# Modulation of a four-block network: sums along features on partitions, with the first block's value projection fed by pairs of features

## The chip, the cores and the metric

The kernel runs on one core of one Trainium2 chip. The metric is the device time of one execution in microseconds (us); the time of the kernel before is the median of three runs, 1766.88 us (1766.28 to 1769.8).

## The reference, cut to what matters

Four blocks (GLA, SGU, FoX, GLA) run over x, 256 tokens by 1024 features; a hybrid block and a PEER feed-forward follow and are not touched. Each of the four blocks is modulated by a vector worked out from a condition c:

```
cond = silu(c)
for i in range(4):
    mod = cond @ w_mod[i] + b_mod[i]          # w_mod[i]: 1024 x 3072
    shift, scale, gate = split(mod, 3)
    h = rms_norm(x, norm_pre_g[i]) * (1 + scale) + shift
    o = mixer_i(h)                            # starts with h @ w_in
    x = x + gate * rms_norm(o, norm_post_g[i])
```

So each block needs three vectors of 1024 (scale and shift at its start, gate at its end), each a product of a 1024-vector with a 1024 x 1024 matrix of 4 MB. Block 0 begins with the values `v = h @ w_v` (1024 x 1024), then keys, part of the gate z, queries, and the rest of z; a decay is worked out from h through a projection of rank 16.

## The kernel before, in words

**Layout.** h is kept with features on partitions, as 8 tiles (kt) of 128 features by 256 tokens. A float32 product is made of three matmuls of float32r parts: a weight tile of 512 KB (`wr`, 4 buffers) is loaded by SP's queue, copied by ScalarE to a high part `wh` (L203), and VectorE subtracts to get the low part `wl` (L204); `hH` and `hL` are the two parts of h. `w_next` hands out the next weight tile of a fixed plan and splits tiles up to five ahead of it (`LEAD`). `w_split` loads the tile four further on (`RAW`).

**Modulation.** `w_mod` is cut into 96 chunks of 512 KB, twelve parts of 8. A chunk has 128 input features on partitions and 1024 outputs along the row. `m_step` (L242) adds one chunk, times one column of silu(c), into an accumulator of 128 x 1024 on VectorE: L255 for the first chunk of a part, L257 for the other seven. The sum over the 128 partitions is left to `m_cols` (L261): four matmuls with ones (L269, each runs as two), a copy to rows on ScalarE (L308), two transposes (L317), and small VectorE operations that add the bias (L275) and apply the norm's gain (L278, L280). The result `modc` has features on partitions, 8 columns.

**Order.** The program writes every engine's queue by hand. `tick()` runs one step of each generator in `tasks`, then of each in `later`; it is called after each block of a projection. In block 0 the 24 chunks for gate 0, scale 1 and shift 1 are spread over the ticks by the list in L636; `m_load` (L240) loads a chunk two ahead, on the SP queue that carries the weights too.

**Start.** The 16 chunks for scale 0 and shift 0 are loaded first (L1502 to L1537), x, the identity and tri in between. `start()` normalises x and transposes it (L365, L371, L1525, L1527). When all 16 are summed and both `m_cols` are through, h is scaled and shifted (L1548 on ScalarE for hH, L1549 on VectorE), L1550 makes hL, and `gla` begins with `proj_tm` for the values: two groups of 512 columns, each over two token blocks with 4 x 6 matmuls (L426 to L428).

**Behind it.** `decay()` (L598) is a task with seven steps: L604 and L606 (rank-16 projection), L613, `log_sigmoid` (L529 to L536), the running sum L617, L619, and exponentials of differences (L622 to L630). It starts at the fourth tick of the value projection. The keys (4 blocks of 24 matmuls, L409 to L411), two blocks of z (silu, L562), and the queries follow; `c_q` (L647) writes a pair of query blocks with the decay's factor `eq`, `k_scale` (L660) scales the keys, and `mix` makes scores (L671, L673, L675) and outputs. `out_proj` (L477) transposes the gate's columns with a broadcast (L492) at its first tick.

```
while have["k"] < 2 * hp + 2 or have["q"] < 2 * hp + 2:
    yield
```

is what holds the scores of a pair of heads (in `mix`).

Of the kernel before, what the change touches and what calls it, by code (L numbers as in the profile page):

```python
# [16 lines left out]
P = 128  # L17
# [27 lines left out]
def _layout():  # L45
    o = 0
    for name, n in [("g_pre", 32), ("g_post", 32), ("b_mod", 96), ("c", 8), ("b_a", 8),
                    ("g_head", 16), ("gate_bias", 16), ("conv_w", 24), ("norm_mix", 8),
                    ("norm_ffn", 8), ("g_q", 1), ("g_k", 1), ("b_f", 1)]:
        COLS[name] = o  # L50
        o += n
    return o
# [11 lines left out]
def _build(ctx, nc, tc, I, out, dbg):  # L64
# [32 lines left out]
    def add(gen, to=tasks):  # L97
        to.append(gen)
# [24 lines left out]
    x = keep.tile([P, NTB, D], F32, name="x")  # L123
    ident = keep.tile([P, P], F32, name="ident")
    tri = const.tile([P, 384], F32, name="tri")
# [14 lines left out]
    sc = const.tile([P, KT], F32, name="sc")  # L140
    act(sc, col("c", 0, 8), AF.Silu)
# [13 lines left out]
    for l in range(4):  # L155
        if l in (0, 3):
            j = l // 3
            plan_tm(I["gla_v"][j], 2)
# [37 lines left out]
    def w_split(i):  # L196
# [10 lines left out]
        w_load(i + RAW)  # L207
# [14 lines left out]
    mods = {}  # L222
    mctx = ExitStack()
    mpool = mctx.enter_context(tc.tile_pool(name="mpool", bufs=3))
    SHIFT, SCALE, GATE = 0, 1, 2
    mplan = [(0, SCALE), (0, SHIFT), (0, GATE), (1, SCALE), (1, SHIFT), (1, GATE), (2, SCALE), (2, SHIFT),
             (2, GATE), (3, SCALE), (3, SHIFT), (3, GATE)]
    mchunks = [(l, part, kt) for l, part in mplan for kt in range(KT)]
    mraw = {}
    nxt_m = [0]  # L230
    MFIRST = 2 * KT

    def m_load(i):
        if i < len(mchunks):
            l, part, kt = mchunks[i]
            if i < MFIRST and i % 2:
# [5 lines left out]
    def m_step():  # L242
# [6 lines left out]
        if kt == 0:  # L249
            mods[l, part, "acc"] = mpool.tile([P, D], F32, tag="macc", name="macc", bufs=2)  # L250
        acc = mods[l, part, "acc"]
        if i >= MFIRST:
            m_load(i + 2)
        if kt == 0:
# [3 lines left out]
        if kt == KT - 1:  # L258
            add(m_cols(l, part), later)

    def m_cols(l, part):  # L261
        acc = mods.pop((l, part, "acc"))
        mc = tiny.tile([P, 8], F32, tag=f"modc{part}", name="modc", bufs=2)
        mods[l, part] = mc
        for _ in range(2 if part == SHIFT else 4):
            yield
        p = pm()
        for g in range(4):
            mm(p[32 * g:32 * g + 32, 0:S], ones[:, 0:32], acc[:, g * S:(g + 1) * S], start=True, stop=True)  # L269
        yield  # L270
        R = rows_copy(p, 4)
        for _ in range(1 if part == SHIFT else 2):
            yield
        pcv = rows_to_cols(p, 4, R)
        tt(mc.rearrange("p (g t) -> p t g", t=2), pcv.rearrange("p t (g r) -> p t g r", r=32)[:, :, :, 0],  # L275
           col("b_mod", l * 24 + part * 8, 8).rearrange("p (g t) -> p t g", t=2), op=ALU.add)
        if part == SCALE:
            stt(mc, mc, 1.0, col("g_pre", l * 8, 8), op0=ALU.add, op1=ALU.mult)  # L278
        elif part == GATE:
            tt(mc, mc, col("g_post", l * 8, 8), op=ALU.mult)  # L280
# [136 lines left out]

    def proj_tm(n, H, L, consume, early=False, late=None):


        def part(p, w, c, tb):
            wh, wl = w
            tsl = slice(tb * P, (tb + 1) * P)
            for k in range(2):
                kt = c * 2 + k
                mm(p, H[:, kt, tsl], wh[:, k], start=(kt == 0), stop=False)  # L426
                mm(p, H[:, kt, tsl], wl[:, k], start=False, stop=False)  # L427
                mm(p, L[:, kt, tsl], wh[:, k], start=False, stop=(kt == KT - 1))  # L428
# [145 lines left out]
    def gla(l, hs, lp, nA, nB, nF):  # L574
# [23 lines left out]
        def decay():  # L598
            for _ in range(3):
# [1083 lines left out]
```

## Time and profile before

| | us |
|---|---|
| median of 3 runs | 1766.88 |
| the profiled execution | 1772.7 |
| its span on the core | 1770.6 |
| TensorE busy | 1682.3 (95%) |
| VectorE busy | 1284.5 (73%) |
| ScalarE busy | 973.6 (55%) |
| low parts of weights, L204 (VectorE, 504 times) | 614.3 |
| modulation chunks of the page's w_mod loads (88 of SP's 512 KB loads) | 5.5 median to landing |

The busy time of TensorE is modelled and pipelined, so 95% is not 95% of its peak. In the profile "idle before <- releaser" names what ended the idle time of the engine just before an instruction. The granted clock is TensorE's, as a share of 2.4 GHz.

### The profile page before, as it was taken

The numbers are of one execution on the slowest core, as the hardware profiler recorded it, in microseconds if no ns is written. First come the engines' busy times: TensorE is split into PE (matmuls) and PEld (weight loads), VectorE is DVE, ScalarE is ACT, GpSimd is POOL, SyncE is SP. The second block draws the span as 40 slices with busy tenths as digits, with TensorE's granted clock in tenths as the row PEclk, the third lists the DMA queues.
The fourth block names the chain that finished last, engine by engine and source line by source line (L and its number), as shares of the span: only waits on it lengthen the run. The fifth ranks groups of instructions, "written<-read, shape, count | busy, mean of one in ns | idle before, by whom it ended". The sixth has DMA issues, their size and how long they took to land.

```text
span 1770.6 us, 28535 instructions
## 1 busy us (share of the span) xinstructions
PE 1682.3 (95%) x10774; PEld 1485.2 (84%) x10774; DVE 1284.5 (73%) x2589; ACT 973.6 (55%) x1531; POOL 60.6 (3%) x102
## 2 busy tenths in 40 slices
PE   3998999999899999989999999999999999999997
PEld 2886886877698788879979999998999888888886
DVE  7888697877786765674576889997774466666665
ACT  3635445655555544435454446668994555555554
POOL 0000000000000000000000000000000000000000
PEclk8999999999999999999999999999999999999999
DMA  8775885853563555334553766664447677777774
GB/s 331 237 270 178 285 308 164 308 194 132 176 202 123 189 179 170 116 106 157 178 193 114 231 215 201 199 188 151 154 153 236 213 243 236 235 236 235 236 235 160
DMA packets 104188, 357.08 MB, mean 202 GB/s; under 512 B 12273, under 2 KB 13297, under 8 KB 103794
## 3 DMA queue, kind: packets, MB, share of 16 engines
q1 hardware_dynamic: 97200, 335.52, 58.8%
q0 software_dynamic: 5120, 16.78, 2.4%
q10 hardware_dynamic: 1730, 2.96, 0.5%
q8 instruction: 85, 1.39, 0.3%
q14 instruction: 53, 0.43, 0.1%
HBM read 337.38 MB, written 17.83 MB: 201 GB/s over the span
## 4 chain that ended last, share of the span: by engine, by line
PE 78%; DVE 12%; ACT 3%; DMA 3%; issue 3%; POOL 0%; SPq 0%; DVEq 0%; POOLq 0%; ACTq 0%
PE pm L1470 20%; PE pj L1447 6%; PE pj L1445 6%; PE pj L1446 6%; PE pj L426 5%; PE pj L428 5%; PE pj L427 5%; DVE wl L204 4%; PE pj L409 4%; PE pj L410 4%; PE pj L411 4%; PE pm L1352 3%; DMA wmod<-in_w_mod 2%; DVE macc L257 2%; ACT wh L203 1%
## 5 line engine op out<-in xcount | busy, mean ns | idle before, releaser
L204 DVE TENSOR_TENSOR wl<-wr,wh 128x1024 fp32r<-128x1024 f32 x504 | 614.3, 1223 | 308.0 <-ACT wh L203 307.1
L203 ACT ACTIVATE wh<-wr 128x1024 fp32r<-128x1024 f32 x504 | 528.2, 1055 | 216.3 <-PE pm L1470 56.0
L1445 PE MATMUL pj<-uH,wh 128*128 128x256 f32 x1024 | 293.8, 287 | 0.0
L1447 PE MATMUL pj<-uL,wh 128*128 128x256 f32 x1024 | 290.0, 283 | 0.0
L1446 PE MATMUL pj<-uH,wl 128*128 128x256 f32 x1024 | 289.9, 283 | 0.0
L409 PE MATMUL pj<-hH,wh 128*128 128x256 f32 x768 | 225.9, 294 | 0.1
L410 PE MATMUL pj<-hH,wl 128*128 128x256 f32 x768 | 221.0, 288 | 3.2 <-DVE wl L204 3.2
L411 PE MATMUL pj<-hL,wh 128*128 128x256 f32 x768 | 220.3, 287 | 0.0
L1470 PE MATMUL pm<-wh 128*128 128x512 f32 x512 | 202.9, 396 | 4.1 <-ACT wh L325 4.1
L1470 PE MATMUL pm<-wl,wh 128*128 128x512 f32 x512 | 202.6, 396 | 0.0
L1470 PE MATMUL pm<-wh,wl 128*128 128x512 f32 x512 | 202.5, 396 | 0.0
L1445 PEld LDWEIGHTS pj<-uH,wh 128*128 128x128 f32 x1024 | 196.7, 192 | 0.0
L1446 PEld LDWEIGHTS pj<-uH,wl 128*128 128x128 f32 x1024 | 196.4, 192 | 0.1
L1447 PEld LDWEIGHTS pj<-uL,wh 128*128 128x128 f32 x1024 | 196.2, 192 | 0.0
L426 PE MATMUL pj<-wh,hH 128*128 128x512 f32 x352 | 144.9, 412 | 15.5 <-DVE hH L392 14.6
L409 PEld LDWEIGHTS pj<-hH,wh 128*128 128x128 f32 x768 | 150.6, 196 | 10.8 <-issue 8.2
L410 PEld LDWEIGHTS pj<-hH,wl 128*128 128x128 f32 x768 | 150.9, 196 | 4.0 <-DVE wl L204 3.9
L411 PEld LDWEIGHTS pj<-hL,wh 128*128 128x128 f32 x768 | 150.6, 196 | 0.0
L427 PE MATMUL pj<-wl,hH 128*128 128x512 f32 x352 | 140.8, 400 | 2.0 <-DVE wl L204 2.0
L428 PE MATMUL pj<-wh,hL 128*128 128x512 f32 x352 | 140.2, 398 | 0.1
L1470 PEld LDWEIGHTS pm<-wh 128*128 128x128 f32 x512 | 96.9, 189 | 26.9 <-ACT wh L325 4.3
L1470 PEld LDWEIGHTS pm<-wh,wl 128*128 128x128 f32 x512 | 96.8, 189 | 22.7 <-DVE wl L326 0.2
(337 smaller groups left out, 2673.7 us busy)
## 6 DMA issues: line engine op xcount, KB each, us to landing
wr<-in_down SPq DMA_DIRECT2D x128, 512.0 KB, 3.8
wr<-in_up SPq DMA_DIRECT2D x128, 512.0 KB, 4.3
wmod<-in_w_mod SPq DMA_DIRECT2D x88, 512.0 KB, 5.5
wr<-in_hyb_fm SPq DMA_DIRECT2D x40, 512.0 KB, 3.5
wr<-in_hyb_qkv SPq DMA_DIRECT2D x36, 512.0 KB, 3.7
spill<-st POOLq DMA_DIRECT2D x64, 256.0 KB, 3.9
a<-spill SPq DMA_DIRECT2D x64, 256.0 KB, 3.2
wr<-in_fox_qkv SPq DMA_DIRECT2D x24, 512.0 KB, 4.5
```

Of the source, the lines that this page charges most:

```text
L203: act(wh, w, AF.Copy)
L204: tt(wl, w, wh.bitcast(F32), op=ALU.subtract)
L409: mm(o, wh[:, kt, cs], H[:, kt], start=(kt == 0), stop=False)
L410: mm(o, wl[:, kt, cs], H[:, kt], start=False, stop=False)
L411: mm(o, wh[:, kt, cs], L[:, kt], start=False, stop=(kt == nk - 1))
L426: mm(p, H[:, kt, tsl], wh[:, k], start=(kt == 0), stop=False)
L427: mm(p, H[:, kt, tsl], wl[:, k], start=False, stop=False)
L428: mm(p, L[:, kt, tsl], wh[:, k], start=False, stop=(kt == KT - 1))
L1445: mm(o, wh[:, kt], uH[:, kt], start=(kt == 0), stop=False)
L1446: mm(o, wl[:, kt], uH[:, kt], start=False, stop=False)
L1447: mm(o, wh[:, kt], uL[:, kt], start=False, stop=(kt == KT - 1))
L1470: mm(acc[tb][n], lw[:, m, tsl], ru[:, 0, HALF[n]], start=(i == 0 and lw is wh and ru is uh), stop=(i == P - 1 and lw is wl))
```

## The change

The modulation is turned round. A chunk of `w_mod` now has 128 output features on partitions and the 1024 inputs along the row (the host lays it out so; its size and its contiguous rows are as before). silu(c) is held as 1024 columns, the same on all 128 partitions, loaded by a broadcast DMA on ScalarE's queue. One `scalar_tensor_tensor` per chunk multiplies and sums along the row (accum_out), and writes one column of the result. `m_cols` with its matmuls, copy and transposes is gone; `m_done` adds the bias and applies the gain.

In the first block the chunks come in the order of four pairs of features: two of scale, two of shift, then the two value-weight tiles (one for each half of the columns) for the same pair. `first_values` replaces the start and the first `proj_tm`: after each pair it scales and shifts two feature tiles (both hH and h on ScalarE), splits two weight tiles, makes hL, and adds the pair's 24 matmuls into four PSUM tiles. x and the identity are loaded ahead of the chunks, tri on ScalarE's queue. `decay()` of block 0 starts at the first tick, which comes behind the values. The list of steps per tick in block 0 changes.

```
+    nc.sync.dma_start(x, I["x"])
+    nc.sync.dma_start(ident, I["ident"])
-    sc = const.tile([P, KT], F32, name="sc")
-    act(sc, col("c", 0, 8), AF.Silu)
+    sc = mpool.tile([P, D], F32, name="sc", bufs=1)
+    nc.scalar.dma_start(sc, I["c"].partition_broadcast(P))
+    act(sc, sc, AF.Silu)
...
-            plan_tm(I["gla_v"][j], 2)
+                plan.extend((I["gla_v"][j][g, c], 2) for c in range(4) for g in range(2))
...
-        w_load(i + RAW)
+        if i < FIRST_W:
+            pump("wr")
+        else:
+            w_load(i + RAW)
...
+    mchunks = [(0, part, 2 * c + i) for c in range(4) for part in (SCALE, SHIFT) for i in range(2)]
+    mchunks += [(l, part, kt) for l, part in mplan for kt in range(KT)]
+    FIRST_M, FIRST_W = 2 * KT, KT
+    queue = [("m", i, "wr" if i % 4 == 3 else "wmod") for i in range(FIRST_M)]
+    for c in range(4):
+        queue[6 * c + 4:6 * c + 4] = [("w", 2 * c + i, "wr") for i in range(2)]
+    queue += [("w", FIRST_W + i, "wr") for i in range(RAW)] + [("m", FIRST_M + i, "wmod") for i in range(2)]
+    free = {"wr": RAW, "wmod": 3}
+    def pump(got=None):
+        if got:
+            free[got] += 1
+        while queue and free[queue[0][2]]:
+            kind, i, pool = queue.pop(0)
+            free[pool] -= 1
+            (m_load if kind == "m" else w_load)(i)
...
-            ts(acc, w, sc[:, 0:1], None, op0=ALU.mult)
-            stt(acc, w, sc[:, kt:kt + 1], acc, op0=ALU.mult, op1=ALU.add)
-            add(m_cols(l, part), later)
+        jk = mpool.tile([P, D], F32, tag="mjk", name="mjk", bufs=1)
+        stt(jk, w, 1.0, sc, op0=ALU.mult, op1=ALU.mult, accum_out=mcols[l, part][:, kt:kt + 1])
+        if i >= FIRST_M:
+            m_load(i + 2)
+            if kt == KT - 1:
+                m_done(l, part)
+        else:
+            pump("wr" if i % 4 == 3 else "wmod")
+
+    def m_done(l, part, k0=0, n=KT):
+        mc = mcols[l, part][:, k0:k0 + n]
+        tt(mc, mc, col("b_mod", l * 24 + part * 8 + k0, n), op=ALU.add)
         if part == SCALE:
+            stt(mc, mc, 1.0, col("g_pre", l * 8 + k0, n), op0=ALU.add, op1=ALU.mult)
         elif part == GATE:
+            tt(mc, mc, col("g_post", l * 8 + k0, n), op=ALU.mult)
...
         def decay():
-            for _ in range(3):
+            for _ in range(3 if l else 0):
                 yield
...
-        add(mod_steps([1] * 8 if l else [0] * 8 + [1] * 8 + [2] * 4 + [1] * 4 + [2] * 2), later)
+        later.append(mod_steps([1] * 8 if l else [1] * 10 + [2, 1] * 3 + [1] * 5))
...
+    def first_values(h, hH, hL, consume):
+        ss = [tiny.tile([P, 2], F32, tag=f"ss{tb}", name="ss") for tb in range(NTB)]
+        for tb in range(NTB):
+            for m in range(2):
+                square_sum(x[:, tb, HALF[m]], ss[tb][:, m:m + 1])
+        r = [inv_rms(ss[tb], "b", ms[tb]) for tb in range(NTB)]
+        m_step()
+        for tb in range(NTB):
+            xn = [work.tile([P, 512], F32, tag="xn", name="xn", bufs=2) for _ in range(2)]
+            ts(xn[0], x[:, tb, HALF[0]], r[tb], None, op0=ALU.mult)
+            act(xn[1], x[:, tb, HALF[1]], AF.Copy, scale=r[tb][:, 0:1])
+            for m in range(2):
+                act(h[:, 4 * m:4 * m + 4, tb * P:(tb + 1) * P], turned(xn[m]), AF.Copy)
+        ps = [[pj(), pj()], [pj(), pm()]]
+        for c in range(4):
+            for _ in range(4 if c else 3):
+                m_step()
+            for part in (SCALE, SHIFT):
+                m_done(0, part, 2 * c, 2)
+            e = slice(2 * c, 2 * c + 2)
+            for d in (hH, h):
+                for kt in range(2 * c, 2 * c + 2):
+                    act(d[:, kt], h[:, kt], AF.Identity, scale=mods[0, SCALE][:, kt:kt + 1],
+                        bias=mods[0, SHIFT][:, kt:kt + 1])
+            w_fill(2 * c + 1)
+            tt(hL[:, e], h[:, e], hH[:, e].bitcast(F32), op=ALU.subtract)
+            w_fill(2 * c + 2)
+            for g in range(2):
+                w = w_next(False)
+                for tb in range(NTB):
+                    tm_part(ps[g][tb], w, hH, hL, c, tb)
+        for g in range(2):
+            for tb in range(NTB):
+                consume(g, tb, ps[g][tb])
         tick()
+        w_fill(FIRST_W + LEAD)
```

`tm_part` is the inner function of `proj_tm`, taken out unchanged.

## Rows read from the trace of the kernel before

**Rows 1.** Windows, block 0: length, busy time of PE, PEld, DVE, ACT, POOL, PEclk, DMA.
```profile
65.60:94.00 28.40, 26.05 (x217) 25.84 (x215) 28.37 (x34) 16.91 (x21) 0.00 (x0) 1.00 0.76 260
94.00:134.00 40.00, 38.86 (x287) 36.00 (x288) 31.25 (x47) 14.30 (x27) 2.13 (x2) 0.91 0.76 263
```

**Rows 2.** Timeline, first scores: start, length, engine, line, operation, idle before.
```profile
93.32 0.68 DVE L647 SCALAR_TENSOR_TENSOR qk<-pj,eq 128x512 f32<-128x512 f32 x1
...
94.15 1.09 PE L671 MATMUL pm<-qk,kk 128*128 128x64 f32 x6 [2.50 <-DVE qk L647]
```

**Rows 3.** Timeline, block 0's out-projection, VectorE and TensorE.
```profile
140.01 0.16 DVE L275 TENSOR_TENSOR modc<-pm,cols 128x8 f32<-128x8 f32 x1
...
140.29 0.42 DVE L554 TENSOR_TENSOR oL<-o,oH 128x256 fp32r<-128x256 f32 x1
...
140.52 1.09 PE L492 MATMUL pm<-ident,modc 128*128 128x128 f32 x4 [3.56 <-DVE modc L280]
```

**Rows 4.** Windows behind the two idle times, columns as in rows 1.
```profile
94.90:101.60 6.70, 6.70 (x33) 6.70 (x33) 5.25 (x7) 0.00 (x0) 0.00 (x0) 0.51 0.99 388
139.30:146.00 6.70, 5.48 (x16) 4.49 (x17) 6.19 (x8) 3.89 (x5) 0.00 (x0) 0.51 0.84 268
```

**Rows 5.** Timeline of TensorE, one part's sum and transposes, and a wait.
```profile
211.92 0.64 PE L269 MATMUL pm<-macc,ones 128*32 128x256 f32 x8
212.49 0.38 PE L409 MATMUL pj<-hH,wh 128*128 128x256 f32 x1
...
222.27 0.38 PE L317 MATMUL pm<-ident,rows 128*128 128x128 f32 x2
222.41 0.36 PE L409 MATMUL pj<-hH,wh 128*128 128x256 f32 x1
...
162.52 0.44 PE L317 MATMUL pm<-ident,rows 128*128 128x128 f32 x2 [0.73 <-ACT rows L308]
```

**Rows 6.** Timeline of the start and of decay's first matmuls.
```profile
11.84 0.63 ACT L352 ACTIVATE jk<-x 128x512 f32<-128x512 f32 x1 [7.36 <-DMA x<-in_x]
...
20.05 1.97 PE L371 MATMUL pm<-ident,xn 128*128 128x128 f32 x8 [20.05 <-DMA wm<-in_w_mod]
...
51.77 1.07 PE L604 MATMUL pm<-h,wal 128*32 128x256 f32 x16
```

**Rows 7.** DMA issues up to 160 us: queue, count, KB each, median us to landing.
```profile
wr<-in_gla_qk SPq DMA_DIRECT2D x8, 512.0 KB, 3.9
...
x<-in_x SPq DMA_DIRECT2D x1, 1024.0 KB, 8.0
```

**Rows 8.** Timeline of VectorE: a modulation step and its successor, an accumulator read.
```profile
86.33 1.28 DVE L257 SCALAR_TENSOR_TENSOR macc<-wmod,sc,macc 128x1024 f32<-128x1024 f32 x1
87.53 1.21 DVE L204 TENSOR_TENSOR wl<-wr,wh 128x1024 fp32r<-128x1024 f32 x1
...
161.14 0.08 DVE L506 DVE_READ_ACCUMULATOR jk<-t,x 128x1 f32 x1
```

**Rows 9.** Timeline: modulated features on ScalarE; value matmuls at full clock.
```profile
36.56 1.59 ACT L1548 ACTIVATE hH<-h,modc 128x256 fp32r<-128x256 f32 x3 [1.04 <-DVE modc L275]
...
47.15 0.39 PE L427 MATMUL pj<-wl,hH 128*128 128x512 f32 x1
47.37 0.39 PE L428 MATMUL pj<-wh,hL 128*128 128x512 f32 x1
```

**Rows 10.** Timeline of ScalarE around the switch from exp to silu.
```profile
77.78 1.05 ACT L203 ACTIVATE wh<-wr 128x1024 fp32r<-128x1024 f32 x1
78.85 1.28 ACT L562 ACT_TABLE_LOAD   x1
80.17 0.38 ACT L562 ACTIVATE zt<-pj 128x256 f32<-128x256 f32 x1
```

**Rows 11.** Groups of VectorE from 57.6 to 94: busy us, mean ns, idle before.
```profile
L204 DVE TENSOR_TENSOR wl<-wr,wh 128x1024 fp32r<-128x1024 f32 x11 | 13.4, 1219 | 1.9 <-ACT wh L203 1.9
...
L255 DVE TENSOR_SCALAR macc<-wmod,sc 128x1024 f32<-128x1024 f32 x1 | 0.7, 746 | 0.0
```

More of the change, by code (lines that the diff above doesn't have):

```diff
@@ L95, in _build, with add @@
     tasks, later = [], []
-    def add(gen, to=tasks):
-        to.append(gen)
+    def add(gen):
+        tasks.append(gen)
     def tick():
@@ L235, in m_load @@
             l, part, kt = mchunks[i]
-            if i < MFIRST and i % 2:
+            if i < FIRST_M and i % 4 == 3:
                 mraw[i] = wpool.tile([P, D], F32, tag="wr", name="wm")
@@ L416, in proj_fm, with tm_part @@
             tick()
+    def tm_part(p, w, H, L, c, tb):
+        wh, wl = w
+        tsl = slice(tb * P, (tb + 1) * P)
+        for k in range(2):
+            kt = c * 2 + k
+            mm(p, H[:, kt, tsl], wh[:, k], start=(kt == 0), stop=False)
+            mm(p, H[:, kt, tsl], wl[:, k], start=False, stop=False)
+            mm(p, L[:, kt, tsl], wh[:, k], start=False, stop=(kt == KT - 1))
     def proj_tm(n, H, L, consume, early=False, late=None):
         def part(p, w, c, tb):
[L422 to L428, printed above, removed]
+            tm_part(p, w, H, L, c, tb)
         for gi in range(n):
@@ L642, in c_v @@
                 nc.vector.tensor_copy(v[:, tb, g * 512:(g + 1) * 512], p)
-        proj_tm(2, hH, hL, c_v, early=True)
+        if l:
+            proj_tm(2, hH, hL, c_v, early=True)
+        else:
+            first_values(h, hH, hL, c_v)
         def c_q(c, p):
@@ L755, in c_v @@
             act(v[:, tb, g * 512:(g + 1) * 512], p, AF.Gelu_apprx_tanh, accum_out=sums[:, tb, g:g + 1])
-        add(mod_steps([1] * 24), later)
+        later.append(mod_steps([1] * 24))
         proj_tm(2, hH, hL, c_v, early=True)
@@ L874, in normed @@
                                         col("g_k" if half else "g_q"), done)
-        add(mod_steps([1, 1, 0] * 8 + [1] * 8), later)
+        later.append(mod_steps([1, 1, 0] * 8 + [1] * 8))
         add(forget())
@@ L1499, in dump @@
             nc.sync.dma_start(out[tb * P:(tb + 1) * P, :], x[:, tb])
-    for i in range(6):
-        m_load(i)
-        if i == 3:
-            nc.sync.dma_start(ident, I["ident"])
-            nc.sync.dma_start(x, I["x"])
-            nc.sync.dma_start(tri, I["tri"])
+    pump()
+    nc.scalar.dma_start(tri, I["tri"])
     hs = new_h(True)
-    h, hH, hL = hs
-    def start():
+    def first_values(h, hH, hL, consume):
         ss = [tiny.tile([P, 2], F32, tag=f"ss{tb}", name="ss") for tb in range(NTB)]
@@ L1522, in start @@
             for m in range(2):
-                d = h[:, 4 * m:4 * m + 4, tb * P:(tb + 1) * P]
-                if m:
-                    nc.vector.tensor_copy(d, turned(xn[m]))
-                else:
-                    act(d, turned(xn[m]), AF.Copy)
-    for i in range(MFIRST):
-        m_step()
-        if i == 5:
-            add(start())
-        tick()
-        if i < MFIRST - 6:
-            m_load(i + 6)
-        elif i % 2 == 0:
-            w_load(i // 2 - MFIRST // 2 + 3)
-    w_load(3)
@@ L1539, in _build @@
-    for i in range(2):
-        m_load(MFIRST + i)
-        w_fill(i + 1)
-    drain()
-    while tick_later():
-        pass
-    A0, B0 = mods[0, SCALE], mods[0, SHIFT]
-    for kt in range(KT):
-        a, b = A0[:, kt:kt + 1], B0[:, kt:kt + 1]
-        act(hH[:, kt], h[:, kt], AF.Identity, scale=a, bias=b)
-        ts(h[:, kt], h[:, kt], a, b, op0=ALU.mult, op1=ALU.add)
-        tt(hL[:, kt], h[:, kt], hH[:, kt].bitcast(F32), op=ALU.subtract)
-        if kt in (2, 5):
-            w_fill(2 + kt // 2)
@@ L1598, in layouts @@
     put("b_mod", colv(g["b_mod"].reshape(-1)))
-    put("c", colv(g["c"].reshape(-1)))
     put("b_a", colv(g["gla_b_a"].reshape(-1)))
```

47 lines of the change are left out of this document (11 added, 36 removed).

## The prediction, made before the change was run

> **What bounds the kernel now.** I read the windows first, then the first 165 us instruction by instruction, then the groups. The windows show where the change can act [rows 1]: from 65.6 to 94 us VectorE works 28.37 of 28.4 us, from 94 to 134 TensorE 38.86 of 40. So the first block is bound by VectorE up to the first scores and by TensorE behind them. The hand-over is one instruction: the first pair of queries is written by VectorE at 93.32, ends at 94.0, and TensorE, idle 2.50 us for it, begins the scores at 94.15 [rows 2]. Whatever moves that write moves everything behind it; that is the term to get right. Behind it three things tie the modulation to TensorE. The out-projection stands 3.56 us for the gate's column (L280), which comes through ones-matmuls, a row copy, transposes and VectorE's queue [rows 3]. After this stall, as after the one at 94, the granted clock is 0.51, that is 1.2 GHz instead of 2.4 [rows 4]. And each of the twelve parts spends TensorE time on L269 and L317 in mid-stream [rows 5].
>
> The profiled execution took 1772.7 us (span 1770.6), 5.8 above the median of 1766.88; the sum is a difference, which I add to the median. About 0.2% (3.5 us) is what a measurement of this kernel tells from no change.
>
> **Part 1: the new start.** x now leads the queue. Before, it stood behind 2 MB of w_mod, took 8.0 us from issue to landing, and ScalarE began on it at 11.84 [rows 6, 7]. That is 3.3 MB at some 0.4 MB per us behind a start of 3.4; with cols (0.1 MB) ahead and the broadcast c (0.5 MB) beside it on ScalarE's queue I put x (1 MB) at 7.9. ScalarE must do the silu of 1024 columns (1.1), a table load (1.3) and four square sums of 0.63, so the sums are there at 11.3, and VectorE, which has their two small operations ahead of its first modulation step, starts that at 11.6. No row shows the broadcast: landing ahead of x it costs nothing and may save 1.3, since ScalarE's silu comes earlier; with a landing as slow as x's before it costs 1.6. I take 0, for it is issued first.
>
> One step becomes scalar_tensor_tensor with a full second operand and an accumulator. The old step is 1.28, its successor starting 1.20 later; reading an accumulator took 0.08 [rows 8]: 1.29. Bounds for the unknown form are 1.20 (no read) and 1.45 (the read exposed with its wait); with 23 of them ahead of the scores that is 2 us less or 3.7 more.
>
> The second token block's scaled half needs the tile that four transposes release (eight took 1.97 [rows 6]): VectorE stands until 14.5. Then three more steps to 18.8, and the pair of features begins its chain: three small operations of 0.16 that follow one another (0.6) [rows 3]; four ScalarE activations of 256, by the row 1.59 for three [rows 9], so about 2.1; one weight copy of 1.05 [rows 10]; the weight's low part (1.22, less the overlap of 0.08 that [rows 8] show between successors: 1.14); hL of 512 columns (half of it, 0.6); the second low part (1.14). VectorE is idle for the 3.2 us in which ScalarE works, because the next steps stand behind the low part in its queue. So a pair takes 5.2 + 0.6 + 3.2 + 2.9 = 11.8, against some 7.5 us that its 3 MB need at that rate: **VectorE's queue, with ScalarE in the middle, sets the pace, not the DMA**. Pair 0 ends at 18.8 + 0.6 + 3.2 + 2.9 = 25.5, pair 3 at 60.9, its hL at 59.8.
>
> TensorE does 24 matmuls per pair, 0.22 apart at full clock [rows 9], twice that at half [rows 4]: 5.4 or 10.2. It rests over 3 us between pairs, and rests of 2.5 and 3.6 us halved the clock before, so the last burst is mixed: 8.0. The values end at 67.8 (65.2 to 70.0); before, about 65.6, with decay's first matmuls inside.
>
> **Part 2: what waits behind the values.** Decay now starts at the tick behind them. ScalarE is held by the last value copy and by al, which needs decay's 16 matmuls (1.07 [rows 6]); then the first key weight: its low part starts at 67.8 + 2.7 = 70.5. VectorE did nothing for most of the 9.6 us before. Five weights are split in a row, and the fifth and sixth are loaded only when the first and second are done (71.6, 72.8): by the row 3.9 to land [rows 7], 1.05 to copy, 1.14 to subtract, so the sixth is through at 78.9. Then decay's first VectorE work, at 57.6 before.
>
> From there to the query write VectorE's order is nearly the old one, and the stretch of 36.4 us (57.6 to 94.0) is my ruler. It holds 11 low parts with 1.9 us of waiting [rows 11] and a value copy of 512 columns. After, seven low parts (-4.6), no wait (-1.9) and no copy (-0.6); seven accumulator reads (+0.6), a 1.28 in place of a 0.75 at the part's first step (+0.5) [rows 8, 11], the gate's two small ones (+0.4). Decay is now spread over the ticks of the key and z blocks, so exp and silu alternate on ScalarE: four more table loads of 1.28. With each 1.34 from the instruction before to the one behind [rows 10], the last exp ends 0.75 after VectorE wants it (+0.7). Sum 31.5: the write ends at 110.4, against 94.0: **+16.4**. TensorE, with nine blocks of 2.9 us and 4 us of first wait, is ready near 99, so the longer idle costs nothing more; the half clock behind it was there before.
>
> The Trainium skill, "ScalarE: Activation LUTs", section What ACT_TABLE_LOAD costs, puts a switch at about 2.66 us, a 1.38 us drain included. The rows speak against it: the copy ends at 78.83, the load starts at 78.85, the silu at 80.17, which leaves no room for a drain [rows 10]. By that page the sum would be 5.5 us more, by the row it is as it stands here.
>
> **Part 3: what goes.** In block 0 behind the scores three ones-matmul groups and three pairs of transposes leave: 0.57 and 0.14 each [rows 5] is 2.1, with 0.7 of waiting for a row copy, and 0.4 where they stood among other small matmuls: -3.2. The gate's column is ready sixteen blocks early, so the 3.56 stall goes, and with it the 6.7 us at half clock, in which 5.48 us of work would have taken 2.7: 6.3 at most. Late next is oL of the last feature, done at 140.7 [rows 3], while TensorE would want it near 142.4: I count 5.5, with 3.6 and 6.3 as ends. Blocks 1 to 3 lose seven parts of 0.71 and a wait of 0.4: -5.4, at least 4 if some of it turns into waits for weights. Against it their steps cost VectorE 56 x 0.09 + 7 x 0.5 = 8.5 us more over 400 in which TensorE leads: 0 to 1.5, I take 0.5. What moves at no cost: tri, wal and wa2 on ScalarE's queue (they are wanted after 67 us; if late, they would hold al). SP's order (w_mod and weights interleaved) lets every chunk land 4 us or more ahead of its step except the two weights priced above.
>
> **Sum:** +16.4 - 3.2 - 5.5 - 5.4 + 0.5 = **+2.8**, so 1769.7, within 0.2% of no change. It stands on a difference of two large terms.
>
> **Rivals.** *VectorE's backlog is larger (slower).* Place: the query write. The first step at 13.2 instead of 11.6 (+1.6), 12.4 us a pair (+2.4), the last burst all at half clock (+2.2) put the write 22.6 later than before, 1775.9. It decides from a delay of 17.1, where the gains of 13.6 and 3.5 us are used up. For it: every added instruction is in one queue. Against: each price is from a row. *The backlog is smaller (faster).* The first step 1.3 earlier, 11.4 a pair (-1.6), the last burst at full clock (-2.6), the two weights in time (-1.6): a delay of 9.3, 1762.6. It decides below 10.1. For it: blocks 1 to 3 and the gate gain in any case. *The table switches cost more where exp and silu alternate.* Were each of the four twice its 1.34 us [rows 10], the last exp and with it the scaling of k would come 5.4 us later: 1775.1. Against: the row of the one switch there is. The skill's section named above speaks for it.
>
> **Numbers.** No change 0.40; faster 0.24; larger backlog 0.32 and table switches 0.04, together slower 0.36. The faster case with the gate's whole 6.3 and no VectorE cost reaches 1761, the slower one with only 3.6 there, 1778; 1760 to 1778 leaves two in ten outside. The likeliest case alone has 1766 to 1773.
>
> **What would show it.** First modulation step near 11.6; pairs 11.8 apart on VectorE with 3.2 us gaps for ScalarE; TensorE in four bursts, values done near 68; the query write near 110 with TensorE idle some 10 us before it; no wait before L492; no L269. I am wrong if the write ends before 104 or after 114, if the pairs are paced by DMA, or if the out-projection stands as before.

## The result, and the profile after

The change made the kernel slower: 1781.51 us median (1777.93 to 1783.13, 4 runs) against 1768.16 (1766.28 to 1769.8, 4 runs), a ratio on record of 1.0055 [1.0037, 1.0073], the brackets being the 95% interval. The two medians alone would give 1.0076, and the record does not say which runs of before the ratio rests on. A repeat (e4 below) gave 1.0039 [1.0026, 1.0051].

Put on the forecast's base of 1766.88, the ratio makes 1776.6 us (1773.4 to 1779.8), 9.7 more than before. The forecast was 1769.7, with 1760 to 1778 as its range. So the time lies inside the range, near its upper end and above the 1766 to 1773 of the likeliest case, while the median of the four runs as it stands is 3.5 above the range. No change, the likeliest case, did not come; the slower one did.

The profiled execution after, 1777.93 with a span of 1775.9, is the shortest of its four; the profiled one of before, 1772.7, lies above all four of its kernel's. So the spans differ by 5.3 us and not by 13.3. The profiles are therefore read stage by stage, and the verdicts come from the ratios.

First the stretch up to the first query write, which answers to [rows 1, 2]. The windows of the kernel before, cut at the start of its scaling and at decay's first VectorE work; the two rows behind them run from the scores to the out-projection and on to block 1. The columns after the length are busy us (and instructions) of each engine, granted clock, DMA share and GB/s:

```profile
core 0: us, PE busy (x) PEld busy (x) DVE busy (x) ACT busy (x) POOL busy (x), PEclk, DMA share, GB/s
0.00:13.20 13.20, 0.00 (x0) 0.00 (x0) 4.90 (x6) 4.14 (x8) 0.76 (x6) 1.00 0.86 325
13.20:57.60 44.40, 27.41 (x121) 19.23 (x122) 36.73 (x50) 18.84 (x30) 2.96 (x4) 0.85 0.84 302
57.60:94.00 36.40, 34.05 (x252) 32.43 (x250) 34.40 (x42) 22.81 (x28) 0.00 (x0) 1.00 0.72 246
...
94.15:133.90 39.75, 38.76 (x287) 35.87 (x287) 31.15 (x47) 14.10 (x27) 2.13 (x2) 0.91 0.76 263
133.90:167.60 33.70, 28.43 (x128) 21.80 (x124) 27.03 (x47) 17.44 (x35) 1.94 (x2) 0.90 0.63 209
```

The same view of the kernel after, cut at the first modulation step, at the end of the last pair's low part, at decay's first VectorE work and at the end of the write:

```profile
0.00:10.79 10.79, 0.00 (x0) 0.00 (x0) 0.64 (x4) 6.34 (x12) 1.81 (x9) 1.00 0.83 293
10.79:58.20 47.41, 30.43 (x92) 21.39 (x93) 33.21 (x59) 19.21 (x30) 1.50 (x1) 0.80 0.78 273
58.20:75.40 17.20, 14.88 (x74) 12.34 (x73) 9.68 (x11) 8.60 (x13) 0.00 (x0) 0.75 0.78 272
75.40:106.30 30.90, 22.60 (x189) 22.39 (x187) 29.72 (x48) 22.17 (x26) 0.00 (x0) 0.91 0.73 243
```

This is a ledger of VectorE: the end of the write is its busy time plus its idle time ahead of it. Before, 76.0 busy and 18.0 idle make 94.0. After, 73.2 busy and 33.1 idle make 106.3. VectorE has 2.8 us less to do and stands idle 15.1 us longer. Of the 33.1 idle, 10.2 lie before the first step, 14.2 in the four pairs, 7.5 while the values end, and 1.2 behind. The timeline of VectorE after shows one pair, and the instructions that close each part:

```profile
start us, us, engine line op out<-in xcount [idle before <-releaser]
32.67 1.23 DVE L212 TENSOR_TENSOR wl<-wr,wh 128x1024 fp32r<-128x1024 f32 x1 [3.09 <-ACT wh L211]
33.81 0.68 DVE L1548 TENSOR_TENSOR hL<-h,hH 128x512 fp32r<-128x512 f32 x1
34.41 1.22 DVE L212 TENSOR_TENSOR wl<-wr,wh 128x1024 fp32r<-128x1024 f32 x1
35.55 1.22 DVE L276 SCALAR_TENSOR_TENSOR mjk<-wmod,sc 128x1024 f32<-128x1024 f32 x1
...
40.76 0.16 DVE L286 TENSOR_TENSOR modc<-modc,cols 128x2 f32<-128x2 f32 x1
44.00 1.22 DVE L212 TENSOR_TENSOR wl<-wr,wh 128x1024 fp32r<-128x1024 f32 x1 [3.09 <-ACT wh L211]
...
75.44 0.87 DVE L546 TENSOR_SCALAR la<-pm,cols 128x256 f32<-128x256 f32 x2
...
98.42 2.30 DVE L677 TENSOR_TENSOR kk<-kk,qk 128x512 f32<-128x512 f32 x5 [1.04 <-ACT kk L644]
...
100.63 1.22 DVE L276 SCALAR_TENSOR_TENSOR mjk<-wmod,sc 128x1024 f32<-128x1024 f32 x1
101.78 0.08 DVE L276 DVE_READ_ACCUMULATOR mjk<-wmod,sc 128x1 f32 x1
101.78 1.22 DVE L212 TENSOR_TENSOR wl<-wr,wh 128x1024 fp32r<-128x1024 f32 x1
...
105.59 0.68 DVE L664 SCALAR_TENSOR_TENSOR qk<-pj,eq 128x512 f32<-128x512 f32 x1
...
164.52 1.23 DVE L276 SCALAR_TENSOR_TENSOR mjk<-wmod,sc 128x1024 f32<-128x1024 f32 x1 [2.77 <-DMA wmod<-in_w_mod]
...
167.01 0.68 DVE L512 TENSOR_TENSOR t<-pj,gate 128x512 f32<-128x512 f32 x1
```

In each pair VectorE sums four chunks, finishes the columns, and then waits 3.09 us (3.15 in the first pair) until ScalarE has scaled the two feature tiles and copied the weight. The next pair's steps stand behind this pair's low parts in its queue. The last rows show what became of the gate's stall [rows 3]. The wait before the transposes of the gate's column is gone, but a modulation step at 164.52 waits 2.77 us for its chunk, and the out-projection's product L512 stands behind it. SP issued that chunk's load at 157.39, right behind a weight's, and the step could start 7.1 us later. TensorE's waits after, from the timeline, where the first row answers to [rows 2]:

```profile
106.42 1.51 PE L688 MATMUL pm<-qk,kk 128*128 128x64 f32 x6 [8.43 <-DVE qk L664]
143.03 0.65 PE L333 MATMUL pm<-ident,rr 128*128 128x128 f32 x4 [1.89 <-POOL rr L311]
167.75 0.50 PE L434 MATMUL pj<-wh,oH 128*128 128x512 f32 x1 [3.52 <-DVE t L512]
176.94 1.12 PE L382 MATMUL pm<-ident,xn 128*128 128x128 f32 x8 [1.79 <-DVE xn L376]
```

Before, the wait for POOL's rows in front of the out-projection was shorter:

```profile
129.65 0.65 PE L322 MATMUL pm<-ident,rr 128*128 128x128 f32 x4 [0.99 <-POOL rr L300]
```

And the windows behind the write, which answer to [rows 4]: a stretch nearly all at half clock, the scores up to the out-projection, and from there to block 1:

```profile
106.42:114.90 8.48, 8.48 (x41) 8.48 (x42) 5.52 (x8) 0.00 (x0) 0.00 (x0) 0.52 0.76 282
106.42:146.40 39.98, 38.09 (x269) 35.95 (x270) 28.68 (x53) 14.28 (x25) 2.13 (x2) 0.90 0.66 223
146.40:179.30 32.90, 26.38 (x115) 20.54 (x113) 27.73 (x54) 17.31 (x34) 1.94 (x2) 0.95 0.64 217
```

Before, the wait at the scores was 2.50 us and 6.8 us of work ran at half clock behind it; now it is 8.43 and 8.2 (of the 8.48 shown, whose mean clock is 0.52). By stages, from the starts of TensorE's work, after against before: the scores begin 12.3 later; scores to out-projection 40.0 against 39.7; out-projection to block 1 32.9 against 33.7; blocks 1 to 3 407.6 against 412.4; the rest 1189.0 against 1190.6. A second profile of each kernel (e4 against e0) has, in the same order: 11.2 later; 40.6 against 40.6; 33.2 against 34.0; 403.8 against 413.3; 1192.6 against 1188.8. The first three differences repeat within about 1 us, the last two scatter by 5.

### The profile page after: what moved, and what is told of

Read it like the earlier page. It is cut to its first block, busy times and chain, and to the rows that moved or that the text cites. A ratio compares the mean times of both kernels' runs of the same rounds, so it can differ in the third digit from the quotient of the medians.

```text
span 1775.9 us, 28374 instructions
## 1 busy us (share of the span) xinstructions
PE 1680.1 (95%) x10654; PEld 1487.1 (84%) x10654; DVE 1281.2 (72%) x2678; ACT 981.0 (55%) x1535; POOL 60.1 (3%) x102
## 4 chain that ended last, share of the span: by engine, by line
PE 78%; DVE 11%; ACT 5%; issue 3%; DMA 3%; POOL 0%; SPq 0%; DVEq 0%; POOLq 0%; ACTq 0%
PE pm L1487 20%; PE pj L1464 6%; PE pj L1463 6%; PE pj L1462 6%; PE pj L434 5%; PE pj L435 5%; PE pj L436 5%; PE pj L420 4%; PE pj L421 4%; PE pj L422 4%; DVE wl L212 4%; PE pm L1369 3%; ACT wh L211 1%; DVE mjk L276 1%; DMA wmod<-in_w_mod 1%
## 5 line engine op out<-in xcount | busy, mean ns | idle before, releaser
L276 DVE SCALAR_TENSOR_TENSOR mjk<-wmod,sc 128x1024 f32<-128x1024 f32 x92 | 112.1, 1218 | 19.1 <-DMA wmod<-in_w_mod 18.7
```

## The experiments

The theory: the turned modulation by itself is a gain, and the new start costs more than that gain, because VectorE waits in it for ScalarE (and for loads) where before it had other work. Its rivals: that the turned step itself is dearer, that the list of steps does it, and, later, that the write is set by decay's chain through ScalarE rather than by VectorE's total. The ratios of e0 to e11 are to the kernel before on the same chip. "Write", "scores" and "block 1" are the starts in the profile, in us; the profiles of e0 and e2 are of the longest execution of each.

| kernel | ratio and interval | write | scores | block 1 |
|---|---|---|---|---|
| e0 before again | 0.9991 [0.9979, 1.0003] | 95.5 | 96.3 | 170.9 |
| after | 1.0055 [1.0037, 1.0073] | 105.6 | 106.4 | 179.3 |
| e4 after again | 1.0039 [1.0026, 1.0051] | 106.8 | 107.6 | 181.4 |
| e1 turned, old start | 0.9958 [0.9941, 0.9974] | 93.5 | 94.4 | 162.0 |
| e7 e1, other list | 0.9954 [0.9941, 0.9967] | 94.0 | 94.8 | 164.5 |
| e10 e1, steps later | 0.9983 [0.9969, 0.9996] | 96.7 | 97.6 | 166.9 |
| e2 next pair's steps ahead | 1.0023 [1.0013, 1.0033] | 101.2 | 102.1 | 173.2 |
| e3 after, other list | 1.0041 [1.0027, 1.0056] | 106.0 | 106.9 | 176.7 |
| e5 e2, loads ahead too | 1.0005 [0.9991, 1.0019] | 98.5 | 99.4 | 170.3 |
| e6 e5, other list | 0.9990 [0.9978, 1.0002] | 98.5 | 99.3 | 168.3 |
| e8 e6, no step before the write | 1.0051 [1.0038, 1.0063] | 96.7 | 97.5 | 179.6 |
| e9 e8, two steps in the last pair | 1.0039 [1.0022, 1.0057] | 95.8 | 96.6 | 175.4 |
| e11 e6, decay first | 0.9977 [0.9966, 0.9988] | 97.0 | 97.9 | 166.7 |

**e0: the kernel before, unchanged.** No edit; it shows how far a run and a profile of the same kernel scatter.

> The kernel before, unchanged, for a profile from the same chip as the runs below. Both theories: within 0.2% of the kernel before; first query write ends near 94 us, block 1 begins near 167.6 us.

The ratio holds 1, and the same program's write began 2.2 us later than in the profile of before (95.5 against 93.3). Block 1 began 3.3 later (170.9 against 167.6). So a shift of 2 or 3 us in one profile is no finding.

**e1: the turned modulation alone**, with the old start, order and list.

```
-        if kt == 0:
-            ts(acc, w, sc[:, 0:1], None, op0=ALU.mult)
-        else:
-            stt(acc, w, sc[:, kt:kt + 1], acc, op0=ALU.mult, op1=ALU.add)
+        stt(jk, w, 1.0, sc, op0=ALU.mult, op1=ALU.mult, accum_out=mcols[l, part][:, kt:kt + 1])
...
-            add(m_cols(l, part), later)
+            m_done(l, part)
```

> Only the turned modulation (multiply and sum along the row, features on partitions, no ones-matmuls or transposes); the start, the order of loads, the value projection and the list of steps are those of before. Theory 'head' (the loss of the change sits in the new start, the turned modulation is a gain): the first query write ends at 91 to 93 us, no wait before L492's transposes, blocks 1 to 3 lose about 0.7 us a part; 1754 to 1762 us, ratio to before 0.992 to 0.997. Rival 'form' (the multiply-and-sum with its accumulator read costs VectorE more than the matmuls cost TensorE): 1768 us or more, ratio 1.000 or above.

0.9958 [0.9941, 0.9974], the first clear gain. It is inside the expected ratio, though the median, 1765.38, and the write, which ended at 94.2, are later than was expected. The windows of e1, cut as those of before, then the scores and the out-projection:

```profile
0.00:13.20 13.20, 0.00 (x0) 0.00 (x0) 5.23 (x10) 3.62 (x3) 0.77 (x6) 1.00 0.86 318
13.20:57.60 44.40, 24.17 (x101) 17.94 (x102) 36.60 (x62) 19.67 (x32) 2.89 (x4) 1.00 0.86 316
57.60:94.20 36.60, 34.10 (x252) 32.45 (x251) 34.57 (x49) 23.39 (x28) 0.00 (x0) 1.00 0.72 244
...
94.40:132.10 37.70, 35.75 (x268) 33.60 (x269) 31.36 (x60) 13.09 (x24) 2.13 (x2) 0.95 0.80 276
132.10:162.00 29.90, 25.12 (x114) 19.33 (x112) 26.56 (x51) 17.16 (x34) 1.94 (x2) 0.99 0.68 229
```

VectorE's ledger is that of before: 76.4 busy, 17.8 idle. The write moves by 0.2. The gain lies behind: scores to out-projection 37.7 against 39.7, and out-projection to block 1 29.9 against 33.7, where the gate's stall was. So the turned step is not what made the kernel slower; what is left is the new start with its list. After against e1 there are 269 and 268 matmuls between scores and out-projection, busy 38.09 and 35.75 at a mean clock of 0.90 and 0.95: those 2.3 us are the clock. They are not shown to come from the new start: e1's 3.4 us at half clock is the shortest there in all fourteen profiles, and e7, with the same start, has 10.2. Even here a new wait stands in the old one's place, 3.33 us for the next block's rows behind the steps in VectorE's queue:

```profile
94.36 0.85 PE L657 MATMUL pm<-qk,kk 128*128 128x64 f32 x6 [2.66 <-DVE qk L633]
...
159.68 1.11 PE L357 MATMUL pm<-ident,xn 128*128 128x128 f32 x8 [3.33 <-DVE xn L351]
```

**e2: the next pair's four steps ahead of this pair's low parts**, so that VectorE has work while ScalarE scales and copies.

```
+        for _ in range(3):
+            m_step()
         for c in range(4):
-            for _ in range(4 if c else 3):
-                m_step()
...
+            for _ in range(4 if c < 3 else 0):
+                m_step()
             w_fill(2 * c + 1)
```

> The changed kernel with one reordering in the start: the four modulation steps of the next pair of features stand in VectorE's queue ahead of this pair's weight low parts, so that they run while ScalarE scales the features and copies the weight. Theory 'head': a pair takes 8.3 us instead of 11.3, the values end at 54 to 56 us instead of 63, the first query write at 96 to 98 instead of 106; 1771 to 1774 us, 0.994 to 0.996 of the changed kernel. Rival 'loads' (a pair is paced by its 3 MB or by TensorE at half clock): a pair stays above 10.5 us and the time within 0.2% of the changed kernel.

1.0023 [1.0013, 1.0033]: the write comes 4.4 us earlier than after, and the gap is gone from all but the last pair, but part of it came back as a wait for loads, so that a pair took 10.7 us (28.91 to 39.59) and not the 8.3 expected. VectorE's timeline in e2:

```profile
28.91 1.23 DVE L276 SCALAR_TENSOR_TENSOR mjk<-wmod,sc 128x1024 f32<-128x1024 f32 x1 [1.66 <-DMA wmod<-in_w_mod]
39.59 1.23 DVE L276 SCALAR_TENSOR_TENSOR mjk<-wmod,sc 128x1024 f32<-128x1024 f32 x1 [2.34 <-DMA wmod<-in_w_mod]
```

In SP's queue the weight loads for a pair, held by their buffers, stood ahead of the chunks that VectorE now wanted first; e5 swaps them.

**e3: the change with no step in the out-projection.**

```
-        later.append(mod_steps([1] * 8 if l else [1] * 10 + [2, 1] * 3 + [1] * 5))
+        later.append(mod_steps([1] * 8 if l else [1] * 10 + [2] * 7))
```

> The changed kernel with another list of steps in block 0: all 24 are done by the last block of z, none is left for the out-projection. Theory 'out-projection' (the wait for the gate's column went, and a modulation step that waits for its load in front of the out-projection's product took its place): the waits of 3.5 and 1.8 us there go, block 1 begins 4 to 5 us earlier, 1776 to 1778 us against 1781. Rival: the three steps moved forward delay the outputs of the heads by as much, block 1 begins within 1 us of the changed kernel.

The wait before L512 went, and the stretch from out-projection to block 1 fell from 32.9 to 28.0. But the stretch in front of it rose from 40.0 to 41.8:

```profile
106.90:148.70 41.80, 38.64 (x269) 36.50 (x270) 31.05 (x57) 14.28 (x25) 2.13 (x2) 0.89 0.72 239
148.70:176.70 28.00, 24.81 (x115) 19.36 (x113) 25.49 (x50) 17.29 (x34) 1.94 (x2) 1.00 0.65 218
```

Block 1 begins 2.6 us earlier than after, less than the 4 to 5 expected, and the ratio, 1.0041, can't be told from e4's 1.0039. The list is at most a small part of the loss.

**e4: the change, unchanged, with e5 to e7 on one chip.**

> The changed kernel, unchanged, beside the runs of this call and for a second profile. Theory 'head': query write again 10 to 13 us later than before, half clock behind the scores for longer than the 6.8 to 10.2 us of before; 1779 to 1783 us, 0.4 to 0.7% above the kernel before. Rival 'one profile deceived' (the query write of the first profile was a chance): the write within 5 us of before.

1778.38 against 1771.66. The write at 106.8 and a half clock of 17.1 us from 100.1 repeat the picture of after.

**e5: e2 with the order of the loads mended as well**: the next pair's chunks ahead of this pair's weights.

```
-        queue[6 * c + 4:6 * c + 4] = [("w", 2 * c + i, "wr") for i in range(2)]
+        o = 6 * c + 4 + 4 * (c < 3)
+        queue[o:o] = [("w", 2 * c + i, "wr") for i in range(2)]
```

> Steps ahead as in the run of that name, and on SP's queue the next pair's chunks of w_mod ahead of this pair's weight tiles. Theory 'queues' (with the steps ahead a pair was held at 10 us because its chunks stood in SP's queue behind weight loads that wait for a buffer): no wait of a modulation step for its load over 1 us, a pair takes 8.2 to 8.8 us, the values end at 52 to 55 us, the query write at 94 to 97; 1766 to 1770 us, within 0.2% of the kernel before. Rival 'bandwidth' (3 MB a pair at what the DMA gives): a pair stays at 9.5 us or more, no gain on the run before it.

A pair takes 8.2 us where no load is late (steps begin at 29.14 and 37.30), against 11.3 after, as expected. The first key block starts at 59.1 instead of 66.2, the write comes at 98.5, and the time, 1771.85, is 6.5 below e4 on the same chip, with intervals that do not touch. That is the cost of VectorE's waits in the pairs, found by taking them away. Write and time are still above the 94 to 97 and 1766 to 1770 expected; a step at 57.97 waits 1.94 for its load. The gap of 3.10 in front of the last pair's low part stays: no next pair is left to fill it.

**e6: e5 with the list of e3.**

> The run before with all 24 steps of block 0 done by the last block of z. If the two effects are separate, another 1.5 to 4 us less: 1763 to 1768 us; if the steps moved forward hold the heads' outputs up, no gain.

1769.72, 8.7 below e4, level with the kernel before: 0.9990 [0.9978, 1.0002]. Against e5 it is 2.1 less, which the intervals can't tell from nothing. Both queues mended, the new start still costs what the turned modulation gains.

**e7: e1 with no step in the out-projection** (`[0] * 8 + [1] * 8 + [2] * 8`).

> The turned modulation with the old start, and no step left for the out-projection of block 0. Theory 'head' with 'out-projection': the 3.3 us wait in front of block 1 goes, out-projection to block 1 in 28 us instead of 29.9: 1761 to 1764 us, the fastest of all, 0.993 to 0.996 of before. Rival: the new start, once mended, is better by its earlier values: then the run before this one is faster than this one.

1763.42 on that chip, 0.9954 [0.9941, 0.9967]. It is the best version of the study together with e1, from which it can't be told. From out-projection to block 1 it takes 26.5, from scores to out-projection 43.2 instead of e1's 37.7: the steps were moved, not saved.

**e8: e6 with gate 0's steps behind the first query write** (`[0] * 9 + [2] * 12`), to see whether VectorE's total sets the write.

> The run with both orders mended (e6_order_and_list), with gate 0's and scale 1's steps moved behind the first query write: nine ticks without a step, then two a tick, so five steps fall into the out-projection. Theory 1 (VectorE's queue sets the query write, TensorE the time behind it): nine steps of 1.27 us, 11.4 us, leave the stretch from the last value copy to the write, which moves from 98.5 to 87 to 91, the wait before the scores falls below 3 us and the half clock behind it gets shorter; the time falls by 3 to 8 us against e6, below the kernel before (ratio 0.992 to 0.997). Theory 2 (ScalarE's exponentials and the loads set it): the write moves by less than 4 us. Theory 3 (the steps must be paid somewhere before block 1): the write comes earlier, but block 1 still starts near 168 behind steps of scale 1 and shift 1 that wait for their loads, and the time is that of e6 within 2 us.

The write moved by 1.8 us only. e6 first, then e8; windows from decay's first VectorE work to the write:

```profile
68.40:99.20 30.80, 22.06 (x184) 21.85 (x183) 29.62 (x48) 21.79 (x25) 0.00 (x0) 0.90 0.72 239
```

```profile
69.40:97.30 27.90, 20.14 (x168) 19.93 (x167) 21.51 (x32) 21.71 (x25) 0.00 (x0) 0.95 0.45 137
```

VectorE's work fell by 8.1 us and its idle time rose from 1.2 to 6.4. The timeline of e8 says for whom it waits then:

```profile
69.44 1.66 DVE L547 TENSOR_SCALAR la<-pm,cols 128x256 f32<-128x256 f32 x4
...
88.11 1.23 DVE L212 TENSOR_TENSOR wl<-wr,wh 128x1024 fp32r<-128x1024 f32 x1 [2.55 <-ACT wh L211]
...
92.18 2.30 DVE L678 TENSOR_TENSOR kk<-kk,qk 128x512 f32<-128x512 f32 x5 [1.83 <-ACT kk L645]
...
96.66 0.68 DVE L665 SCALAR_TENSOR_TENSOR qk<-pj,eq 128x512 f32<-128x512 f32 x1
...
158.78 1.23 DVE L277 SCALAR_TENSOR_TENSOR mjk<-wmod,sc 128x1024 f32<-128x1024 f32 x1 [1.45 <-DMA wmod<-in_w_mod]
161.00 1.22 DVE L277 SCALAR_TENSOR_TENSOR mjk<-wmod,sc 128x1024 f32<-128x1024 f32 x1 [1.00 <-DMA wmod<-in_w_mod]
```

So theory 2 of the expectation holds for the write, a second limit close below the first: ScalarE's queue with its four table loads. Theory 3 had the mechanism of the time but not its size: two steps a tick in the out-projection wait for their loads, TensorE waits 1.89, 4.38 and 2.13 us there, block 1 begins at 179.6, 11.3 later than in e6, and the ratio is 1.0051 against 0.9990, where the expectation had the time of e6 within 2 us.

**e9: e8 with two of gate 0's steps in the last pair's gap**, and their loads ahead of the key weights; the list is `[0] * 9 + [2] * 11`.

```
+    queue += [("m", FIRST_M + i, "wmod") for i in range(2)]
+    queue += [("w", FIRST_W + i, "wr") for i in range(RAW)]
...
-            for _ in range(4 if c < 3 else 0):
+            for _ in range(4 if c < 3 else 2):
```

> As e8, and the first two steps of gate 0 stand ahead of the last pair's low parts, where VectorE waits 3.10 us for ScalarE in e6; their two loads go ahead of the key weights in the queue. Theory 1: the two steps cost nothing in that gap (values end as before, within 0.6 us), so 2.5 us of VectorE's work leaves the stretch behind the values; as e8 has already no step in front of the query write, the write stays within 1 us of e8's, and only the steps behind the scores get fewer: 0 to 3 us less than e8. Rival: the two loads in front of the key weights delay these by 2.6 us (two of 512 KB at some 0.4 MB per us), and the query write comes 2 to 3 us later than in e8.

The write came 0.9 earlier than in e8, the first key block 1.1 earlier, block 1 4.2 earlier; the intervals, 1.0051 [1.0038, 1.0063] and 1.0039 [1.0022, 1.0057], overlap. The rival, key weights delayed by those loads, did not show.

**e10: e7 with the steps later still** (`[0] * 12 + [2] * 12`).

> The turned modulation with the old start (e7_old_start_list), with twelve ticks without a step and then two a tick. In e7 some six to eight steps of 1.27 us stand ahead of the query write at 94.0. Theory 1 (VectorE's queue sets the write): it moves to 85 to 90, unless TensorE's blocks, which began at 35.7, then lead; the time falls by 3 to 7 us against e7, to a ratio of 0.990 to 0.994. If the new start is worth something once the steps are out of the way, e8 comes out at or below this run; if the new start is a loss in itself, e8 stays 5 us or more above it. Rival: steps behind the scores wait for loads and the block's end is late again, so the time is e7's within 2 us.

Worse than e7, 0.9983 [0.9969, 0.9996]; the write went back to 96.7. A chunk is loaded two steps ahead, so two steps in one tick catch up with their loads (VectorE's timeline):

```profile
88.78 1.22 DVE L253 SCALAR_TENSOR_TENSOR mjk<-wmod,sc 128x1024 f32<-128x1024 f32 x1 [2.18 <-DMA wmod<-in_w_mod]
```

The list didn't do what it was meant to: six of e7's seven steps still stand in front of the write, two a tick, and now wait. So this run doesn't test VectorE's total with the old start. By the expectation's other rule the new start is a loss in itself, since e8 came out 10.4 us above this run. But that pair is not clean, as e8's steps also hold up its out-projection (block 1 at 179.6 against 166.9). The clean pair is e6 against e7, both with no step there and on one chip: 0.9990 [0.9978, 1.0002] against 0.9954 [0.9941, 0.9967], 6.3 us.

**e11: e6 with decay ahead of most key weights.**

```
         tick()
+        w_fill(FIRST_W + 1)
+        tick()
+        w_fill(FIRST_W + 3)
+        tick()
         w_fill(FIRST_W + LEAD)
```

> The run with both orders mended (e6_order_and_list), with two more ticks between the first splits of key weights, so that the decay's second projection and its logarithm stand ahead of most of these weights. Theory 4 (in the new start the decay's chain through ScalarE and VectorE, from its first VectorE work at 68.4 in e6 to the write 30.1 us later, sets the first query write, because it begins only behind the values and behind four copies of key weights): the first decay work on VectorE moves from 68.4 to 60 to 62, fewer switches between the two tables stand in ScalarE's queue, and the write moves from 98.5 to 89 to 93; the time falls by 4 to 9 us against e6, to a ratio of 0.994 to 0.997. Theory 1 (VectorE's total work before the write sets it): the order of the work does not matter as long as VectorE is busy; the write stays within 2 us of 98.5 less the waits it loses. Rival: the key blocks now wait for their weights, TensorE loses what the decay gains, and the scores begin within 2 us of e6.

Decay's first VectorE work came at 59.9 instead of 68.4, three of the four table loads went, and the write moved by 1.5 us:

```profile
59.91 1.65 DVE L547 TENSOR_SCALAR la<-pm,cols 128x256 f32<-128x256 f32 x4
...
97.05 0.68 DVE L665 SCALAR_TENSOR_TENSOR qk<-pj,eq 128x512 f32<-128x512 f32 x1
```

And its windows over that stretch:

```profile
60.00:97.70 37.70, 28.06 (x215) 27.45 (x215) 35.34 (x52) 23.30 (x28) 0.00 (x0) 0.92 0.77 249
```

VectorE is idle there for 2.4 us of 37.7: now its work sets the write. e8 took away the work and left decay's chain, e11 took away the chain's wait and left the work. Each moved the write by under 2 us, no more than e0's scatter, where over 5 had been expected; the idle times, 6.4 and 2.4, say that the two limits lie that close together. The ledger up to the write is 72.9 busy and 24.8 idle, 7.0 more idle than e1, nearly all of it before 60 us; no run tested that part. By its median e11 is the best version with the new start, 0.9977 [0.9966, 0.9988], though its interval overlaps e6's. It is still behind e7, and by its median behind e1. Both edits together were not tried.

## Where the prediction was right, and where it was wrong

**The new start (+16.4 predicted, +12.3 measured).** The mechanism was right in each part, and each part was somewhat too dear. The first step came at 10.79 (11.6 said; the silu and its table load were over at 7.9, before ScalarE began on x at 8.07), pairs were 11.3 apart (11.8) with gaps of 3.09 to 3.15 (3.2), TensorE ran in four bursts, the first key's low part stood at 66.2 (70.5), the sixth was through at 75.5 after waits of 1.34 and 0.90 for late weights (78.9). From decay's first VectorE work to the end of the write it took 30.8 against 31.5. The write ended at 106.3, inside the 104 to 114 that the prediction had set itself. e2 and e5 confirm the cause: giving VectorE the next pair's steps in the gap, and the loads that go with them, took 7.1 us off the write (8.2 against e4's) and 6.5 off the time.

**Table switches (+0.7 in the sum).** There are four more, as said, and the wait for the last exponential was 1.04. ScalarE's timeline after shows what one costs:

```profile
88.70 1.28 ACT L576 ACT_TABLE_LOAD   x1
90.00 0.38 ACT L576 ACTIVATE zt<-pj 128x256 f32<-128x256 f32 x1
90.40 1.28 ACT L644 ACT_TABLE_LOAD   x1
91.69 1.68 ACT L644 ACTIVATE kk<-kk 128x256 f32<-128x256 f32 x3
```

From a load's start to the next activation it is 1.30 and 1.29, against 1.32 in [rows 10], and the rival of twice that falls. The Trainium skill, "ScalarE: Activation LUTs", section What ACT_TABLE_LOAD costs, has 2.66 with a drain; in none of these rows is there a drain.

**"The half clock behind it was there before" (priced at nothing).** This held within the scatter. TensorE's wait grew from 2.50 to 8.43, but behind its restart 8.2 us ran at half clock, against 6.8 in the profile of before and 8.7 in e0, the same kernel. In the pair of profiles compared here that is 0.7 us of time.

**The matmuls, copies and transposes that leave (-3.2).** This step failed in what it made of the work, not in the work. About half of it stood in front of the out-projection and half in it. With the part at half clock counted at full clock (an estimate from each window's busy time and clock), TensorE's busy time fell by 1.3 in the one and 1.1 in the other, near the 2.5 that the matmuls were priced at. But scores to out-projection came out 0.2 longer, and no shorter in e4 against e0. The clock took 0.7 of the 1.3, and the wait for POOL's rows, 1.89 in place of 0.99, another 0.9: the work that left had partly stood ahead of a wait that remains.

**The gate's stall (-5.5).** This is the largest miss. The stall before L492 went, as predicted, but the stretch from out-projection to block 1 fell by 0.8 only, in both pairs of profiles: TensorE's busy time there fell by 2.05 (28.43 to 26.38) and its idle time rose by 1.25 (5.27 to 6.52). So the prediction's third sign of being wrong, an out-projection that stands as before, came nearly true. It named oL as late next, and took 5.5 of 6.3 for it, though by its own figures oL was there (140.7) before it was wanted (142.4); late next was VectorE's product L512, 3.52 us, behind a step that waited for its chunk. The prediction had said that SP's order lets every chunk land 4 us or more ahead of its step, and had followed the gate's own chunks only to the gate. This is the step that failed: the chunk for the step at 164.52 came 2.77 late, issued behind a weight. e3, which keeps steps out of the out-projection, has that stretch at 28.0, 5.7 below before and near the predicted 5.5, and gives 1.8 back in front of it.

**Blocks 1 to 3 (-4.9 net).** Measured -4.8 in this pair of profiles and -9.5 in e4 against e0. The twelve profiles with the turned modulation have 403.8 to 415.4, 408.8 in the mean; the two without have 412.4 and 413.3. So about 4 is what these profiles support, and the agreement to 0.1 is chance.

**The sum.** The terms behind the write were to give back 13.6 and gave 5.4, and the delay, which the sum had made too large by 4.1, made up for half of that. That the time still lies inside the range is therefore in part luck: two misses of opposite sign. The rival with the slower time, a larger backlog on VectorE, is not what happened: its write was to come 22.6 later, and its point of decision was 17.1. The write came 12.3 later, less than the forecast itself had, and with 5.4 given back the point of decision is 8.9. The range took the gate's gain as 3.6 to 6.3; with a gain of nothing as the lower bound its upper end would have been 1781.6.

## What to carry to other kernels

When a product is cut into pieces so that two engines hand each piece back and forth, queue the next piece's work (and its loads) ahead of this piece's second half; otherwise each hand-over is an idle gap of the busier engine, here 3.1 us four times. Add up busy and idle time of the engine that makes the hand-over instruction, up to that instruction: the new start lowered VectorE's busy time by 2.8 us and lost 15.1 in idle time. A change with two independent halves is best measured half by half: the turned modulation alone gains 0.42%, the new start loses more than that. And when a stall is priced as gone, follow what stands behind it in every queue, loads included: the next wait, here 3.52 us, can take its place.

## What the runs showed of the hardware

The stretch at 1.2 GHz (granted clock 0.50) around TensorE's wait for the first scores was longer where the wait was longer. Behind waits of 2.50 and 2.66 us it was 6.8 (before) and 3.4 (e1); with 3.24 to 7.96 it was 10.2 (e7, e0, e10, e11, e8); with 8.20 to 8.87, 13.7 (e9, after, e6); with 9.49 to 9.70, 17.1 (e4, e2, e3, e5). But more of it then lies inside the wait, 5.5 of the 13.7 in after. The part behind the restart, which slows work down, was 3.4 in e1, 6.8 in before, and 7.2 to 9.6 in the other twelve, with no order by the wait: 8.9 behind 3.24 (e7), 7.5 behind 8.87 (e6). So the work at half clock behind a stall of 3.24 us was no less than behind one of 8.43.

The accumulator's read was nearly free. A multiply with a sum along 1024 columns takes VectorE 1.22 us and the read 0.08. Step on step they are 1.26 apart (35.55 to 36.81), inside the bounds of 1.20 and 1.45 that the prediction gave; in front of a low part, where nearly all of gate 0's steps stand, the next instruction starts 1.15 behind (100.63 to 101.78), less than the 1.20 of the step it replaced [rows 8]. The seven reads that the sum priced at 0.6 cost nothing there.

The broadcast of 4 KB to 128 partitions on ScalarE's queue, a shape that no row of before showed, cost nothing either: ScalarE began on it at 5.53, and on x at 8.07.
